# Three engines of a hybrid decoder layer put in written order while its mixers run

## The chip, the cores and the metric

One core of one Trainium2 chip runs one launch of the kernel. The metric is device time in microseconds. A profile of one execution stands beside the times.

## The reference

The layer works on 2048 tokens of width 1024 in float32. Cut to what matters:

```python
hn = rms_norm(h, pre_mix_norm)
proj = hn @ w_in                      # q, k, v, z, a, b of DeltaNet; f, i, q, g of HGRN2
q, k, v = silu(causal_conv4(qkv))     # then l2norm of q and k
o_a = gated_delta_rule(q, k, v, g_dec, beta)     # 4 heads of 128, chunks of 64
o_b = hgrn2(silu(q_hg), (1 - lb) * sigmoid(-f), i_hg, log_f)   # 4 heads, chunks of 16
mix = concat(head_norm(o_a) * silu(z), head_norm(o_b) * silu(g))
h = h + rms_norm(mix @ w_out)
h = h + rms_norm(square(relu(rms_norm(h) @ w_up)) @ w_down)
h = h + rms_norm(p @ w_ple_proj) * sigmoid(h @ w_gate)
```

## The kernel before, in words

Every float32 operand of a big matmul is split into two parts (`split`, L163: a copy on ScalarE at L165, a difference on VectorE at L166), and three products of the parts make one matmul of full precision.

The function `trunk` has four stretches. The first (L361 to L404) multiplies half of the tokens' embeddings p by w_ple (`embed_tile`, L297), stores the tiles (L304, `ed`), and makes the split operands xt of the first quarter of the tokens. The second, the mixers (L407 to L1084), is what the change touches. The third is the output projection, and the fourth the MLP and the gated embedding; in both TensorE runs one long list of matmuls (L1102 and others).

In the mixers the tokens are cut into 4 quarters q of 512. For each quarter TensorE runs 33 *works* (L1019 to L1038): `ab` (the decays and betas of all heads) and, for each of 4 heads, 8 projections of 128 columns. A work is 24 matmuls of 128x512 (L1033) on a weight tile w, and is cut into 3 *ticks* of 8 matmuls. All that the mixers do besides is written as Python generators: `gdn_mixer` (DeltaNet), `hgrn_mixer`, `conv_silu`, `finish` (head norm), `x_scale` and `load_x` (the next quarter's operands, with the split), `decays`, `down_sums` (sums of weights for the MLP). Tables of numbers (`A_STEPS`, `B_STEPS` and others, L51 to L67) say at which tick, or half tick, a generator is resumed; `tick()` (L349) and `half()` (L354) resume what the agenda holds. One head has a period of 24 ticks. What a generator issues between two yields therefore stands, in the program as written, between two groups of matmuls.

The kernel is built under a scheduler that can reorder each engine's instructions. TensorE is in written order for the whole kernel (L306, `tc.manual_schedule`), and so is SyncE, which issues the DMAs, inside the first stretch (L361) and the works' loop (L1013). Before the change ScalarE, VectorE and GpSimd are ordered by the scheduler everywhere: it may take an instruction whose operands are ready ahead of one that was written earlier.

The names that the steps below use:

- DeltaNet, one head: `e_g` (L590, VectorE) and its exponentials (L588, L592, L593, ScalarE) give the decay matrix of the *next* head, while the *previous* head's chain over 4 chunks runs: psa (L735, TensorE), r_g (L737, VectorE), psb (L740, TensorE), w_g (L742, ScalarE), psc (L745, TensorE), S_g (L747, VectorE), then psa of the next chunk.
- The *solve* (L669, L672, L674, VectorE): 32 rows of small triangular systems, two rows at a step of three instructions, each of which needs the one before; two steps are written per tick.
- Its inverse is then doubled in size: xn_g (L688, VectorE), psp_g (L693, TensorE).
- HGRN2: qk_h, att_h, gg_h (L791 to L837, VectorE), keys_h (L829, ScalarE), at_h (L824, TensorE), S_h (L851, VectorE), pss_h (L849, TensorE).
- Ahead of the works' loop stand memsets of the mixers' tiles on VectorE: bound (L419), um, part and xt_full (L424), eight states S (L428).
- `decays` (L465) makes gb from the work `ab` and, by way of gbb (L487) and ps_gb (L490), the columns that the DeltaNet heads need.
- For q = 0 each weight tile is loaded into one of two buffers `raw` (L455), split, and kept in DRAM (L181); later quarters reload it already split (L186).
- At a change of quarter, 9 ticks ahead of it, `load_x` (L944 on) scales (L954) and splits eight tiles xt; the work `ab` of the next quarter and its `decays` follow.
- After the last work (L1041 to L1043) two tiles w_pleb of w_ple and four operands pT (two tiles for each of the quarters 2 and 3, loaded through two buffers `ld` of the pool m2) are made, and 16 more embed tiles (mme, L192) fill TensorE while the last head's mixers end (L1046 to L1084).

Of the kernel before, what the change touches and what calls it, by code (L numbers as in the profile page):

```python
# [84 lines left out]
def trunk(ctx, tc, x, xT, pT, vecs, w_in, w_ab, gdn_a_log, gdn_dt_bias, w_out, w_up, w_down,  # L85
# [321 lines left out]
    with mixers as mctx:  # L407
        mp = mctx.enter_context(tc.tile_pool(name="mp", bufs=1))
        m2 = mctx.enter_context(tc.tile_pool(name="m2", bufs=2))

        def flat(t):
            return t.rearrange("p a b -> p (a b)")
# [1338 lines left out]
```

## Time and profile before

| | us |
|---|---|
| median of 3 runs | 2759.96 |
| lowest and highest run | 2754.35 and 2760.57 |
| profiled execution, its own time | 2759.13 |
| its span | 2757.3 |
| TensorE busy in the span | 2673.0 |
| VectorE busy | 2046.0 |
| ScalarE busy | 1469.8 |
| GpSimd busy | 104.2 |

The span runs from the first to the last instruction that the profiler recorded; 1.8 us of the execution's own time lie around it. A busy time is the union of an engine's recorded instructions, so overlapping ones count once. In rows of a timeline the first number is the start in us from the span's start, the second the time taken; in square brackets stand the engine's idle time ahead of that instruction and what ended it. The mixers lie between about 45 and 1100 us of the span.

### The profile page before, as it was taken

The numbers are of one execution on the slowest core, as the hardware profiler recorded it, in microseconds if no ns is written. First come the engines' busy times: TensorE is split into PE (matmuls) and PEld (weight loads), VectorE is DVE, ScalarE is ACT, GpSimd is POOL, SyncE is SP. The second block draws the span as 40 slices with busy tenths as digits, with TensorE's granted clock in tenths as the row PEclk, the third lists the DMA queues.
The fourth block names the chain that finished last, engine by engine and source line by source line (L and its number), as shares of the span: only waits on it lengthen the run. The fifth ranks groups of instructions, "written<-read, shape, count | busy, mean of one in ns | idle before, by whom it ended". The sixth has DMA issues, their size and how long they took to land.

```text
span 2757.3 us, 38414 instructions
## 1 busy us (share of the span) xinstructions
PE 2673.0 (97%) x12745; PEld 2221.0 (81%) x12745; DVE 2046.0 (74%) x4245; ACT 1469.8 (53%) x2944; POOL 104.2 (4%) x104
## 2 busy tenths in 40 slices
PE   7999999999999999999899999999999999999999
PEld 5788788888888888777788887887888888887887
DVE  6788877787778777577888867767787765567776
ACT  6665554455546445666555645555455555465421
POOL 0000000000000000000000000001000000001000
PEclk9999999999999999999999999999999999999999
DMA  7776776666766665787466547667464446577664
GB/s 263 260 245 219 233 250 221 222 219 233 239 213 217 200 213 169 260 302 238 160 226 220 187 146 253 220 196 244 148 216 139 158 167 209 192 253 244 208 210 133
DMA packets 268742, 589.24 MB, mean 214 GB/s; under 512 B 55658, under 2 KB 60232, under 8 KB 249344
## 3 DMA queue, kind: packets, MB, share of 16 engines
q1 hardware_dynamic: 268544, 586.79, 63.7%
q8 instruction: 101, 1.65, 0.3%
q14 instruction: 97, 0.79, 0.1%
HBM read 419.75 MB, written 166.92 MB: 213 GB/s over the span
## 4 chain that ended last, share of the span: by engine, by line
PE 63%; DVE 10%; DMA 8%; issue 5%; ACT 4%; SPq 1%; POOL 1%; DVEq 0%; POOLq 0%; ACTq 0%
PE u L1102 21%; PE d L1102 19%; PE mm L1033 11%; PE mmg L1102 6%; DMA ud_g<-u_g 1%; DMA sys_g<-ud_g 1%; PE mmo L1102 1%; DVE pr_g L669 1%; DVE xs_g L672 1%; DMA raw_out<-in_w_out_dram 1%; DVE xs_g L674 1%; DVE raw_xt L954 1%; DMA db<-hid 1%; DVE xt L166 1%; DMA b<-h1d 1%
## 5 line engine op out<-in xcount | busy, mean ns | idle before, releaser
L1033 PE MATMUL mm<-xt,w 128*128 128x512 f32 x3072 | 785.5, 402 | 1.3 <-ACT zt_zg L548 0.7
L1033 PEld LDWEIGHTS mm<-xt,w 128*128 128x128 f32 x3072 | 558.8, 190 | 107.0 <-ACT zt_zg L548 1.1
L1102 PE MATMUL d<-db,da 128*128 128x512 f32 x2688 | 613.5, 390 | 5.8 <-DVE db L219 3.2
L1102 PE MATMUL u<-t,wu 128*128 128x512 f32 x2604 | 593.3, 390 | 3.5 <-ACT wu L165 3.4
L1102 PEld LDWEIGHTS d<-db,da 128*128 128x128 f32 x2688 | 503.9, 188 | 114.7 <-DVE db L219 6.3
L1102 PEld LDWEIGHTS u<-t,wu 128*128 128x128 f32 x2604 | 489.6, 188 | 106.5 <-ACT wu L165 4.2
L219 DVE TENSOR_TENSOR db<-db 128x512 fp32r<-128x512 f32 x224 | 161.5, 721 | 76.7 <-ACT db L218 75.8
L1431 DVE TENSOR_TENSOR u<-u,u 128x512 f32<-128x512 f32 x224 | 150.7, 684 | 60.0 <-PE u L1102 58.1
L218 ACT ACTIVATE db<-db 128x512 fp32r<-128x512 f32 x224 | 140.8, 629 | 85.1 <-DMA db<-hid 81.8
L1102 PE MATMUL mmo<-mixT,w_out 128*128 128x512 f32 x720 | 170.5, 398 | 9.7 <-DVE w_out L166 6.2
L1102 PE MATMUL mmg<-h2T,wg 128*128 128x512 f32 (+1 forms) x792 | 174.7, 383 | 0.0
L1102 PEld LDWEIGHTS mmo<-mixT,w_out 128*128 128x128 f32 x720 | 137.8, 192 | 41.3 <-DVE w_out L166 7.9
L1102 PEld LDWEIGHTS mmg<-h2T,wg 128*128 128x128 f32 x792 | 145.5, 188 | 29.1
L1472 ACT ACTIVATE u<-u 128x512 f32<-128x512 f32 x128 | 80.9, 632 | 165.1 <-DVE u L1431 164.7
L166 DVE TENSOR_TENSOR da<-da 128x512 fp32r<-128x512 f32 x128 | 93.0, 726 | 87.2 <-ACT da L165 86.8
L165 ACT ACTIVATE da<-da 128x512 fp32r<-128x512 f32 x128 | 80.5, 629 | 135.6 <-DMA da<-sumd 109.8
L165 ACT ACTIVATE wu<-a 128x512 fp32r<-128x512 f32 x124 | 73.9, 622 | 53.0 <-DMA a<-in_w_up_dram 50.2
L669 DVE TENSOR_TENSOR pr_g<-xs_g,sys_g 128x16 f32<-128x16 f32 (+14 forms) x240 | 93.9, 391 | 5.4
L229 POOL TENSOR_TENSOR acc_y<-acc_y,sq_y 128x512 f32<-128x512 f32 x28 | 38.4, 1370 | 1381.7 <-ACT sq_y L228 1381.7
L166 DVE TENSOR_TENSOR wu<-a,wu 128x512 fp32r<-128x512 f32 x124 | 85.0, 688 | 4.3 <-ACT wu L165 4.3
L1473 ACT ACTIVATE u<-u 128x512 f32<-128x512 f32 x128 | 80.8, 631 | 3.7
L166 DVE TENSOR_TENSOR da<-dr,da 128x512 fp32r<-128x512 f32 x96 | 66.3, 690 | 17.6 <-ACT da L165 15.4
(374 smaller groups left out, 3810.9 us busy)
## 6 DMA issues: line engine op xcount, KB each, us to landing
w<-cache_in SPq DMA_DIRECT2D x96, 1024.0 KB
db<-hid SPq DMA_DIRECT2D x224, 256.0 KB
cache_in<-w SPq DMA_DIRECT2D x32, 1024.0 KB
hid<-u SPq DMA_DIRECT2D x128, 256.0 KB
da<-sumd SPq DMA_DIRECT2D x128, 256.0 KB
a<-in_w_up_dram SPq DMA_DIRECT2D x124, 256.0 KB
hid<-ht SPq DMA_DIRECT2D x96, 256.0 KB
dr<-in_w_down_dram SPq DMA_DIRECT2D x96, 256.0 KB
```

Source lines behind the costliest of these rows:

```text
L165: S.activation(t[:, 0], raw, AF.Copy)
L166: eng.tensor_tensor(t[:, 1], raw, t[:, 0], ALU.subtract)
L218: S.activation(t[:, 0], plain(t), AF.Copy)
L219: V.tensor_tensor(t[:, 1], plain(t), t[:, 0], ALU.subtract)
L229: eng.tensor_tensor(acc, acc, sq, ALU.add)
L669: V.tensor_tensor(pr[:, :, :, 0:i], xs[:, None, :, 0:i].broadcast_to([P, 2, GC, i]), sys[:, 0:i, i : i + 2].rearrange("p j two -> p two j" ...
L672: V.tensor_reduce(xs[:, :, i : i + 2].rearrange("p g two -> p two g"), pr[:, :, :, 0 : i + 1], AX.X, ALU.add)
L1033: PE.matmul(ps, *terms[i], start=i == 0, stop=i == nt - 1)
L1102: PE.matmul(ps, a, b, start=start, stop=stop)
L1431: V.tensor_tensor(c[new], c[old], ps, ALU.add)
L1472: S.activation(c[k], c[k], AF.Relu)
L1473: S.activation(c[k], c[k], AF.Square)
```

## The change

The three engines are put in written order from the opening of the mixers' pools to the end of the mixers, which is where the `with` of `mctx` closes:

```diff
     with mixers as mctx:
         mp = mctx.enter_context(tc.tile_pool(name="mp", bufs=1))
         m2 = mctx.enter_context(tc.tile_pool(name="m2", bufs=2))
+
+        mctx.enter_context(tc.manual_schedule(
+            engines={mybir.EngineType.DVE, mybir.EngineType.Activation, mybir.EngineType.Pool}))
 
         def flat(t):
             return t.rearrange("p a b -> p (a b)")
```

Line numbers of the changed kernel are larger by 3 from there on. TensorE's order of 11707 rows is the same; of VectorE's 4247 instructions 2433 stand elsewhere, by 8 places in the mean, and of ScalarE's 2854 there are 1113, by 1.4 places in the mean. Outside the mixers the three engines are still ordered by the scheduler. No instruction is added or taken away.

Three places on VectorE show what moves. The first is the opening of the mixers. Before, VectorE has the split of w_ab0 (the weights of the first work) among the operands of the embed tiles:

```order
L166 TENSOR_TENSOR w_plea1_346<-raw_plea1_253,w_plea1_346 128x512
L229 TENSOR_TENSOR acc_e1_364<-acc_e1_364,sq_e1_1_380 128x512
L166 TENSOR_TENSOR w_ab0_589<-raw_ab0_585,w_ab0_589 128x1024
L207 SCALAR_TENSOR_TENSOR xraw_255<-xraw_255,cols_92,rsb_x0_353 128x512 x3
L166 TENSOR_TENSOR xt0_0_368<-xraw_255,xt0_0_368 128x512
L166 TENSOR_TENSOR xt0_1_385<-xraw_255,xt0_1_385 128x512
```

In the changed kernel VectorE has it behind the last embed row (L229) and all of the memsets, with the splits of the second and third weight tile and of the norm's operand hl_e0 after it:

```order
L229 TENSOR_TENSOR acc_e1_364<-acc_e1_364,sq_e1_7_538 128x512
L422 MEMSET bound_557 128x36
L427 MEMSET um5_559 128x256
...
L431 MEMSET S6_0_581 128x128
L431 MEMSET S7_0_583 128x128
L166 TENSOR_TENSOR w_ab0_591<-raw_ab0_587,w_ab0_591 128x1024
L166 TENSOR_TENSOR w_4_0_0_596<-raw_4_0_0_589,w_4_0_0_596 128x1024
L166 TENSOR_TENSOR w_0_0_0_599<-raw_0_0_0_594,w_0_0_0_599 128x1024
L166 TENSOR_TENSOR hl_e0_615<-acc_e0_288,hl_e0_615 128x512
L474 MEMSET gb_0_640 36x512
```

The three weight splits moved from ahead of the memsets to behind them, and hl_e0 moved behind all three. On SyncE the loads of w_0_0_0's and w_8_0_0's raw tiles and the store of w_ab moved behind the last of the 16 stores of `ed`.

The second place is one head of the steady part, the last head of quarter 2, where VectorE's e_g2_3 belongs to the next DeltaNet head and S_h2_1 is the state of an HGRN2 head. Before, on VectorE:

```order
L669 TENSOR_TENSOR pr_g2_2_7993<-xs_g2_2_7994,sys_g2_2_7948 128x8x12
L587 TENSOR_TENSOR tail_g2_3_8049<-gf_g2_3_8001,gcol_2_6278 128x4
L590 TENSOR_TENSOR e_g2_3_8053<-gf_g2_3_8001,cst_89 128x512
L851 SCALAR_TENSOR_TENSOR S_h2_1_0_8038<-S_h1_1_3_5306,gg_h2_1_6_7940,pss_h2_1_0_8036 128x128
L672 TENSOR_REDUCE xs_g2_2_7994<-pr_g2_2_7993 128x2x4
L674 SCALAR_TENSOR_TENSOR xs_g2_2_7994<-xs_g2_2_7994,sys_g2_2_7948 128x4
```

In the changed kernel VectorE has there:

```order
L675 TENSOR_REDUCE xs_g2_2_7996<-pr_g2_2_7995 128x2x4
L677 SCALAR_TENSOR_TENSOR xs_g2_2_7996<-xs_g2_2_7996,sys_g2_2_7950 128x4
L672 TENSOR_TENSOR pr_g2_2_7995<-xs_g2_2_7996,sys_g2_2_7950 128x8x10
L675 TENSOR_REDUCE xs_g2_2_7996<-pr_g2_2_7995 128x2x4
L677 SCALAR_TENSOR_TENSOR xs_g2_2_7996<-xs_g2_2_7996,sys_g2_2_7950 128x4
L590 TENSOR_TENSOR tail_g2_3_8051<-gf_g2_3_8003,gcol_2_6280 128x4
L593 TENSOR_TENSOR e_g2_3_8055<-gf_g2_3_8003,cst_89 128x512
L750 SCALAR_TENSOR_TENSOR S_g2_1_1_8080<-S_g2_1_0_7984,cd_g2_1_6703,psc_g2_1_1_8078 128x128
L854 SCALAR_TENSOR_TENSOR S_h2_1_1_8086<-S_h2_1_0_8040,gg_h2_1_6_7942,pss_h2_1_1_8084 128x128
```

Tail and e_g moved from ahead of S_h of chunk 0 to behind it and behind the solve steps of their own tick (up to row 10 of the system); S_g and S_h of chunk 1 now stand ahead of the next solve steps.

The third place is the end of the last work. Before, VectorE has the splits of w_pleb and pT among the solve of the last head (pr_g3_3, xs_g3_3), for example:

```order
L674 SCALAR_TENSOR_TENSOR xs_g3_3_11454<-xs_g3_3_11454,sys_g3_3_11408 128x4
L166 TENSOR_TENSOR w_pleb0_11663<-raw_pleb0_11639,w_pleb0_11663 128x512
L669 TENSOR_TENSOR pr_g3_3_11453<-xs_g3_3_11454,sys_g3_3_11408 128x8x16
L166 TENSOR_TENSOR w_pleb0_11663<-raw_pleb0_11639,w_pleb0_11663 128x512
L851 SCALAR_TENSOR_TENSOR S_h3_2_0_11494<-S_h2_2_3_8811,gg_h3_2_6_11400,pss_h3_2_0_11492 128x128
```

In the changed kernel VectorE has all eight of them in one piece, behind the last r_g of head 2 and the solve's last steps:

```order
L740 SCALAR_TENSOR_TENSOR r_g3_2_3_11631<-vt_g3_2_10695,inv_g3_2_10517,psa_g3_2_3_11629 128x128
...
L677 SCALAR_TENSOR_TENSOR xs_g3_3_11456<-xs_g3_3_11456,sys_g3_3_11410 128x4
L672 TENSOR_TENSOR pr_g3_3_11455<-xs_g3_3_11456,sys_g3_3_11410 128x8x30
L675 TENSOR_REDUCE xs_g3_3_11456<-pr_g3_3_11455 128x2x4
L677 SCALAR_TENSOR_TENSOR xs_g3_3_11456<-xs_g3_3_11456,sys_g3_3_11410 128x4
L166 TENSOR_TENSOR pT2_0_11647<-raw_pT2_0_11645,pT2_0_11647 128x512
L166 TENSOR_TENSOR pT2_1_11652<-raw_pT2_1_11650,pT2_1_11652 128x512
L166 TENSOR_TENSOR pT3_0_11657<-raw_pT3_0_11655,pT3_0_11657 128x512
L166 TENSOR_TENSOR pT3_1_11662<-raw_pT3_1_11660,pT3_1_11662 128x512
L166 TENSOR_TENSOR w_pleb0_11665<-raw_pleb0_11641,w_pleb0_11665 128x512 x2
L166 TENSOR_TENSOR w_pleb1_11670<-raw_pleb1_11643,w_pleb1_11670 128x512 x2
```

The four pT splits and the four half splits of w_pleb moved behind r_g of chunk 3, whose psa TensorE issues after its last in-projection matmul, and the order among them turned: pT first, w_pleb last.

## The prediction

> **What bounds the kernel now.** The page's busy times come first, then its chain of work that ended last, then a table of the mixers by stretches, then what TensorE waited for between 64 and 1150 us.
>
> ```profile
> PE 2673.0 (97%) x12745; PEld 2221.0 (81%) x12745; DVE 2046.0 (74%) x4245; ACT 1469.8 (53%) x2944; POOL 104.2 (4%) x104
> PE 63%; DVE 10%; DMA 8%; issue 5%; ACT 4%; SPq 1%; POOL 1%; DVEq 0%; POOLq 0%; ACTq 0%
> 64.00:1087.00 1023.00, 996.75 (x5389) 846.70 (x5390) 784.44 (x2250) 550.32 (x1418) 55.66 (x64) 0.99 0.68 226
> PE psc_g L745 <- ACT w_g L742: 14.9, 13, 4.5
> PE psp_g L693 <- DVE xn_g L688: 5.0, 4, 2.1
> PE psa_g L735 <- DVE S_g L747: 3.6, 4, 1.9
> PE ps_gb L490 <- DVE gbb L487: 2.8, 1, 2.8
> PE at_h L824 <- ACT keys_h L829: 2.3, 3, 0.9
> ```
>
> TensorE is busy for 97% of the span and carries 63% of the last chain. The third line is the steady part of the mixers: of 1023 us TensorE is busy for 996.8, VectorE for 784.4, ScalarE for 550.3. So TensorE bounds, and only 26.2 us of idle time are there to be won. The waits below it say which chains come late: above all psc for ScalarE's w_g, once per DeltaNet head. TensorE's order does not change, so the new order of the others can act in one way only: it makes TensorE wait at other places, or for other lengths. VectorE has about 24% of slack in this stretch as a mean. The question is where it has none.
>
> **The start.** The timeline around the first mixer work:
>
> ```profile
> 39.45 1.21 DVE L166 TENSOR_TENSOR w<-raw,w 128x1024 fp32r<-128x1024 f32 x1
> 44.81 1.62 SPq L304 DMA_DIRECT2D ed<-e  x2
> 45.32 5.74 PE L1033 MATMUL mm_ab<-xt,w_ab 128*128 128x512 f32 x24 [0.31 <-ACT sq_e L228]
> 51.23 0.09 DVE L419 MEMSET bound<- 128x36 f32 x1 [2.06 <-DMA ed<-e]
> 52.93 1.15 DVE L428 MEMSET S<- 128x128 f32 x8
> 52.66 0.33 SPq L456 DMA_DIRECT2D raw<-in_w_in_dram  x1
> 59.75 1.04 ACT L165 ACTIVATE w<-raw 128x1024 fp32r<-128x1024 f32 x1
> ```
>
> TensorE goes from the embed tiles into mm_ab at 45.32 almost without a pause (0.31), because w_ab was split long before. The memsets begin at 51.23, since their memory is free only when the last embed store has landed, and end at 52.93 + 1.15 = 54.08, so they take 2.85. In the new order the split of w_ab stands behind them. The last two stores are issued from 44.81 to 46.43; they may land sooner than 51.2, as weight loads and a store of w_ab no longer go ahead of them. I put the first memset midway between 46.4 and 51.2, at 48.8. Then w_ab is split at 48.8 + 2.85 + 1.2 = 52.85, and mm_ab begins **7.5 us late** (5.1 to 9.9 by the two ends). Behind it on VectorE stands the split of w_0_0_0, whose load can start only when w_ab has left its buffer, at 52.85, and behind that hl_e, which TensorE wants right after mm_ab, at 52.85 + 5.74 = 58.6. From a load's issue at 52.66 to its copy at 59.75 there are 7.1 us, so a load takes between 0 and 7.1; I take 4. With 1.04 for the copy, 1.21 for the split and 0.7 for hl_e it is 59.8: 1.2 more (0 to 4.3). With the clock (below, 1.7) the start costs **+10.4**, between 5 and 16.
>
> **The clock.** A wait also costs time after it:
>
> ```profile
> 319.70 0.71 PE L693 MATMUL psp_g<-xn_g,um 128*128 128x128 f32 x4 [2.10 <-DVE xn_g L688]
> 320.00:322.00 2.00, 2.00 (x13) 0.63 1.31 51
> 322.00:324.00 2.00, 2.00 (x6) 0.52 0.37 141
> 428.02 0.80 PE L745 MATMUL psc_g<-w_g,kt_g 128*128 128x128 f32 x2 [4.55 <-ACT w_g L742]
> ```
>
> The longest wait was that of psc at 428.02, 4.55 us. But already after one of 2.10 us the granted clock was 0.63 and then 0.52 for two stretches of 2 us: 2 x 0.37 + 2 x 0.48 = 1.7 us of work lost. I charge 1.7 to a long wait, and to a part of those near 2 us. The Trainium skill, "TensorE: Matmul & The Clock Gate", section "HAM oscillation — how this bites in real kernels", puts the abstract rule at no idle gaps of TensorE over about 3.4 us. The trace differs, since here 2.10 us were enough. By that rule the six charges of 1.7 that stand on waits of 2 to 3 us below would fall away, and the sum would come out at about 2808.
>
> **The steady heads.** The last head of quarter 2 in the timeline:
>
> ```profile
> 750.24 0.31 DVE L669 TENSOR_TENSOR pr_g<-xs_g,sys_g 128x80 f32<-128x80 f32 x1
> 751.13 0.33 DVE L669 TENSOR_TENSOR pr_g<-xs_g,sys_g 128x96 f32<-128x96 f32 x1
> 751.45 0.68 DVE L590 TENSOR_TENSOR e_g<-gf_g,cst 128x512 f32<-128x512 f32 x1
> 752.06 0.34 DVE L851 SCALAR_TENSOR_TENSOR S_h<-S_h,gg_h,pss_h 128x128 f32<-128x128 f32 x1
> 752.17 1.28 ACT L592 ACTIVATE e_g<-e_g,gcol 128x128 f32<-128x128 f32 x4 [0.40 <-DVE e_g L590]
> 753.88 0.34 ACT L742 ACTIVATE w_g<-psb_g,cc_g 128x128 f32<-128x128 f32 x1
> 754.28 0.49 PE L745 MATMUL psc_g<-w_g,kt_g 128*128 128x128 f32 x2 [0.56 <-ACT w_g L742]
> ```
>
> VectorE's e_g at 751.45 releases four exponentials on ScalarE; w_g stands behind them in ScalarE's queue, and psc came 0.56 late for it. In the new order e_g stands behind S_h and two solve steps of its own tick. A step takes 751.13 - 750.24 = 0.89, so e_g can come up to 1.8 later, and psc with it; where VectorE had idled and does the steps sooner, nothing is lost. I take 1.2 for each of 12 heads (it is nearer to the full delay, as the solve is what VectorE does at that time), 14.4, and 1.7 of clock in three of them: **+19**, between 0 and 12 x (1.8 + 1.7) = 42.
>
> In return S_g and S_h of the next chunk stand ahead of solve steps. What that can bring is bounded by the waits of psa for S_g (3.6), of psp for xn (5.0) and of at_h for keys (2.3), 10.9 in all. I take half, **-6**.
>
> **The three changes of quarter.** A table by stretches of 12 us around the first full one:
>
> ```profile
> 276.00:288.00 12.00, 10.48 (x57) 8.34 (x55) 7.96 (x30) 3.65 (x8) 0.00 (x0) 1.00 0.87 283
> 288.00:300.00 12.00, 11.64 (x68) 9.56 (x67) 11.90 (x32) 6.36 (x15) 0.00 (x0) 1.00 0.70 221
> 300.00:312.00 12.00, 12.00 (x59) 9.87 (x57) 12.00 (x33) 4.83 (x11) 0.00 (x0) 1.00 0.76 239
> 312.00:324.00 12.00, 9.90 (x46) 7.91 (x46) 8.79 (x26) 8.62 (x16) 1.01 (x1) 0.86 0.65 153
> ```
>
> Here VectorE has no slack: 11.90 and 12.00 of 12 us are busy (third column of busy times), with the scale and split of eight tiles xt beside the solve. The scheduler had a choice of what to let wait; in written order an xt split, a solve step and an r_g each wait for all that was written ahead, and in 312 to 324 the decays' chain between VectorE and ScalarE (8.79 and 8.62 busy) blocks what stands behind it. In 276 to 288 VectorE idles for 4.0 us. If work that it ran ahead there returns to its place, the backlog is 4 us larger, and the idle 3.2 us of 312 to 324 lie inside chains that now can't be filled. I take 5.3 of additional wait and 1.7 of clock: 7 for each of three changes, **+21**. The ends are 0 (TensorE's tolerance of a tick or two takes it up) and 15 each (twice the 7.3 us that VectorE idles in these rows: once lost where it had run ahead, once more in the chains), 45.
>
> **The end.** The timeline at the last in-projection work:
>
> ```profile
> 1065.42 12.96 SPq L205 DMA_DIRECT2D raw_pT<-in_pT_dram  x3
> 1076.24 0.69 DVE L166 TENSOR_TENSOR pT<-raw_pT,pT 128x512 fp32r<-128x512 f32 x1
> 1080.82 1.33 ACT L165 ACTIVATE pT<-raw_pT 128x512 fp32r<-128x512 f32 x2
> 1085.54 2.07 PE L1033 MATMUL mm<-xt,w 128*128 128x512 f32 x8
> 1087.45 0.38 PE L735 MATMUL psa_g<-S_g,y_kg 128*128 128x128 f32 x2
> 1087.59 1.63 PE L192 MATMUL mme<-pT,w_pleb 128*128 128x512 f32 x6
> 1089.58 0.60 DVE L669 TENSOR_TENSOR pr_g<-xs_g,sys_g 128x240 f32<-128x240 f32 x1
> 1090.09 0.35 DVE L737 SCALAR_TENSOR_TENSOR r_g<-vt_g,inv_g,psa_g 128x128 f32<-128x128 f32 x1
> ```
>
> The first embed matmul follows at 1087.59 without a wait: pT and w_pleb had been split since 1071. In the new order they stand behind r_g, which needs psa of 1087.45. So r_g ends at 1087.45 + 0.38 + 0.35 = 1088.2. Two solve steps at full width follow: 0.89 each above at an L669 of 0.31, here 0.60, so about 1.25 each, until 1090.7. Two splits of pT2 at 0.66 end at 1092.0. Only they free the buffers for the other two loads; the last issue ended at 1065.42 + 12.96 = 1078.38 and the copies began at 1080.82, so a load takes at most 2.4. I take 2.2: 1094.2, then ScalarE's copy 0.65, the split 0.7, and two half splits of w_pleb0 at 0.7: 1097.0. That is 9.4 us after 1087.59, and 1.7 of clock: **+11**, between 7 (the loads hidden) and 14 (VectorE late by one more tick of 2.1). The 16 embed tiles behind it share two buffers and two engines with the last head's chain in written places; I put **+3** on them, from -5 to +10.
>
> **The sum.** 10.4 + 19 - 6 + 21 + 11 + 3 = 58.4. The profiled execution took 2759.1 (its span of 2757.3 and 1.8 around it), 0.8 below the median of the runs. Its time and the sum give 2817.5, rounded to **2818**. GpSimd's 104 us are on no queue that matters here, and its order moves hardly at all; I charge nothing.
>
> **Rivals.** *Only the two ends cost.* The steady part holds because TensorE asks for results a tick or two after they are written, and VectorE's mean load of 784 in 1023 leaves 24%. For it: most waits before are under 2 us. Against it: the two rows with VectorE at 11.90 and 12.00 of 12. It gives 2759 + 10.4 + 11 = **2780**.
>
> *The lag feeds on itself.* Every head's psc comes the full 1.8 late and falls to half clock, 42, and the quarter changes cost their 45. For it: psc already waits in 13 places and once for 4.5. Against it: a longer wait of TensorE also gives VectorE time to catch up. It gives 2759 + 10 + 42 + 45 + 11 + 3, **2870**.
>
> *Faster.* VectorE's own order decides: S_g and r_g ahead of the solve end the chain that TensorE waits for. Most that this can bring is the idle 26.2 us of the steady part and, by its mean granted clock of 0.99, some 10 us of half clock. It decides if the store of the last embed tile lands before 46, so that mm_ab waits little, and if VectorE is never a tick behind. With both ends charged it gives 2759 - 36 + 21 = **2744**. Against it: psc, over half of the waits listed, waits for e_g, which moved later, not earlier.
>
> **How the numbers follow.** The forecast, all stretches a little slower, has 0.55; only the ends 0.20; the self-feeding lag 0.12; faster 0.07; and 0.06 that gains and losses cancel. A difference of 0.3%, 8.3 us, is about what a measurement of this kernel can tell from none. So slower 0.87, within it 0.06, faster 0.07. The range takes the forecast's bounds and the second case in, and the third at its edge: from 2772, which leaves room below 2780 for the lower ends of start and end (5 + 7), to 2870.
>
> **What would show it.** The first matmul of mm_ab would wait 5 to 10 us for VectorE's split of w, and in VectorE's row ahead of it the memsets would stand. The first mme behind the last mm would wait for pT or w_pleb, by about 9 us. The total of psc behind w_g would go from 14.9 to about 30; TensorE would wait for r_g, xn or gbb at the three changes of quarter, where now one wait of 2.1 stands; and more stretches would show a granted clock near 0.5. If psc's total stays near 15, the steady term is wrong; if the mixers grow by less than 25 us between their first and last mm, the quarter changes are. It would all be wrong if VectorE's waits show that the scheduler's own order had been what delayed r_g and S_g.

## The result and the profile after

The changed kernel took 2921.22 us (median of 4 runs, 2917.42 to 2927.46) against 2757.87 (4 runs, 2754.35 to 2760.57): a ratio of **1.0597**, 95% interval 1.0579 to 1.0614 (the quotient of the two medians is 1.0592). The direction was forecast, the size was not: 163 us instead of 58, and outside the range.

The profiled execution has a span of 2925.2 us, 167.9 longer. Its busy times:

```profile
PE 2725.2 (93%) x12745; PEld 2253.7 (77%) x12745; DVE 2075.5 (71%) x4245; ACT 1463.7 (50%) x2944; POOL 103.7 (4%) x104
```

TensorE has the same 12745 matmuls, but is busy for 52.2 us longer (2673.0 before): the same work at a lower clock. The other 115.7 us are idle time.

As TensorE's order is the same in all kernels here, its n-th matmul can be set against the n-th of the kernel before, and the growth of the difference of their starts says in which stretch time was lost. The profiled executions give, in us lost per stretch (borders in us of before: *start* ends at 84; *quarter* is 290 to 324, 558 to 589 and 818 to 848, about the three changes of quarter; *steady* is what lies between these, up to 1088; *first mme* is the step from the psa behind the last in-projection matmul to the second embed matmul, so that a wait of either of the first two embed matmuls falls in it; *tail* are the 55 us behind that):

| | start, to 84 | steady | quarter | first mme | tail | rest, 1143 on | sum |
|---|---|---|---|---|---|---|---|
| forecast | 10.4 | 13 | 21 | 11 | 3 | 0 | 58.4 |
| the change | 10.6 | 87.5 | 36.4 | 10.3 | 24.8 | -1.3 | 168.2 |

Start and first mme came out as worked out. Nearly all of the error is the steady heads, the tail and a part of the quarter changes. What TensorE waited for, in the whole changed kernel (waits that were as long before are left out):

```profile
PE psc_g L748 <- ACT w_g L745: 49.1, 21, 6.1
PE ps_gb L493 <- DVE gbb L490: 13.2, 4, 3.6
PE at_h L827 <- ACT keys_h L832: 12.9, 9, 7.6
PE psp_g L696 <- DVE xn_g L691: 10.9, 5, 2.6
PE psb_g L743 <- DVE r_g L740: 10.5, 7, 2.6
PE mme L192 <- ACT w_pleb L165: 9.8, 1, 9.8
PE t_hkh L546 <- DVE qk_h L829: 8.0, 1, 8.0
PE mm_ab L1036 <- DVE w_ab L166: 6.4, 1, 6.4
```

Psc's wait for w_g has gone from 14.9 to 49.1 and is still the largest, but seven others together are larger (71.7), and most of these hardly existed before. The start in the timeline:

```profile
44.83 0.73 PE L1036 MATMUL mm_ab<-xt,w_ab 128*128 128x512 f32 x2 [0.35 <-ACT sq_e L228]
47.59 0.09 DVE L422 MEMSET bound<- 128x36 f32 x1 [0.73 <-DMA ed<-e]
50.75 1.16 DVE L166 TENSOR_TENSOR w_ab<-raw_ab,w_ab 128x1024 fp32r<-128x1024 f32 x1
51.97 7.80 PE L1036 MATMUL mm_ab<-xt,w_ab 128*128 128x512 f32 x22 [6.41 <-DVE w_ab L166]
```

Two matmuls of mm_ab, which need only w's first part, go through; the third waits 6.41 for VectorE's split, and the memsets stand ahead of the split, as forecast. They began at 47.59, sooner than the 48.8 that I took. The other 22 matmuls of mm_ab took 7.80, where all 24 had taken 5.74 before.

The steady head that the forecast priced, the last of quarter 2, in the timeline of the changed kernel:

```profile
849.16 0.68 DVE L593 TENSOR_TENSOR e_g<-gf_g,cst 128x512 f32<-128x512 f32 x1
849.88 1.28 ACT L595 ACTIVATE e_g<-e_g,gcol 128x128 f32<-128x128 f32 x4 [0.40 <-DVE e_g L593]
851.58 0.35 ACT L745 ACTIVATE w_g<-psb_g,cc_g 128x128 f32<-128x128 f32 x1
851.98 0.49 PE L748 MATMUL psc_g<-w_g,kt_g 128*128 128x128 f32 x2 [2.26 <-ACT w_g L745]
852.51 0.35 DVE L750 SCALAR_TENSOR_TENSOR S_g<-S_g,cd_g,psc_g 128x128 f32<-128x128 f32 x1 [2.66 <-PE psc_g L748]
```

The chain is closed: e_g late on VectorE, four exponentials and gf on ScalarE, w_g behind them, psc behind w_g, and VectorE itself idle for 2.66 with S_g, with the next solve steps ready behind it. Before, this psc had waited 0.56, so that it waits 1.70 longer. The same wait of 2.26 stands in six heads (psc at 415.23, 488.53, 714.69, 851.98, 1011.39 and 1146.00). In one of them it is a gain: the psc of 488.53 is the one that had waited 4.55 before. And it did not always cost the clock: behind four of the six the granted clock was at 0.50 within 1.5 us, as behind 415.23, while behind 488.53 and 1011.39 it stayed at 1.00 (TensorE's busy time, then the granted clock):

```profile
416.00:419.00 3.00, 3.00 (x10) 0.50 0.02 8
489.00:494.00 5.00, 5.00 (x33) 1.00 0.31 84
```

The four steady stretches as a whole, before and after:

```profile
84.00:290.00 206.00, 197.61 (x1055) 1.00 0.74 245
324.00:558.00 234.00, 226.24 (x1232) 0.99 0.70 234
589.00:818.00 229.00, 226.31 (x1250) 1.00 0.69 233
848.00:1087.00 239.00, 236.16 (x1298) 0.99 0.64 214
```

```profile
94.00:326.00 232.00, 207.86 (x1059) 0.95 0.67 219
371.00:623.00 252.00, 230.84 (x1228) 0.97 0.63 211
667.00:922.00 255.00, 237.97 (x1252) 0.96 0.61 206
965.00:1222.00 257.00, 243.96 (x1301) 0.97 0.58 189
```

The same matmuls, to within five, take 920.6 us of busy time instead of 886.3, so **34 us of the steady loss are the clock**, at a mean of 0.95 to 0.97; the idle time went from 21.7 to 75.4, which is the other 54.

A change of quarter, the first of three alike:

```profile
355.96 1.28 ACT L479 ACT_TABLE_LOAD   x1
357.92 0.68 DVE L480 SCALAR_TENSOR_TENSOR sp<-sp,se 4x512 f32<-4x512 f32 x1 [2.78 <-ACT se L479]
360.49 0.42 DVE L691 STREAM_TRANSPOSE xn_g<-xt_g 128x256 f32<-128x256 f32 x1
360.96 1.12 PE L696 MATMUL psp_g<-xn_g,um 128*128 128x128 f32 x4 [2.59 <-DVE xn_g L691]
366.77 0.28 DVE L490 COPY gbb<-gb 36x256 f32<-36x256 f32 x1
367.11 0.32 PE L493 MATMUL ps_gb<-cst,gbb 36*128 36x36 f32 x1 [3.05 <-DVE gbb L490]
```

```profile
355.00:361.00 6.00, 3.41 (x16) 1.00 0.01 2
361.00:371.00 10.00, 6.45 (x20) 0.51 0.80 236
```

VectorE stands 2.78 us with sp, for ScalarE's exponential and logarithm, and 1.28 of this is the ACT_TABLE_LOAD that ScalarE has between the two; xn, which needs neither, stands behind it, and TensorE waits 2.59 for xn, runs at half clock, and waits 3.05 for gbb, which is a short copy behind a convolution and steps of an HGRN2 head. The tail:

```profile
1232.04 2.93 PE L192 MATMUL mme<-pT,w_pleb 128*128 128x512 f32 x6 [9.75 <-ACT w_pleb L165]
1244.31 0.63 ACT L218 ACTIVATE mixT<-mixT 128x512 fp32r<-128x512 f32 x1 [5.74 <-DMA mixT<-mixd]
1250.45 0.42 ACT L832 ACTIVATE keys_h<-qk_h 128x256 f32<-128x256 f32 x1 [1.95 <-DVE qk_h L829]
1250.92 1.22 PE L827 MATMUL at_h<-qk_h,keys_h 128*128 128x128 f32 x4 [7.59 <-ACT keys_h L832]
```

The first embed matmul waits 9.75 (forecast 9.4). Then ScalarE stands 5.74 us with the copy of a mixT tile whose load was issued in the same step, and the last head's keys, in the same queue, come 7.59 late.

### The profile page after: what moved, and what is told of

Its sections match the earlier page's. It is cut to its first block, busy times and chain, and to the rows that moved or that the text cites. A ratio compares the mean times of both kernels' runs of the same rounds, so it can differ in the third digit from the quotient of the medians.

```text
span 2925.2 us, 38388 instructions
## 1 busy us (share of the span) xinstructions
PE 2725.2 (93%) x12745; PEld 2253.7 (77%) x12745; DVE 2075.5 (71%) x4245; ACT 1463.7 (50%) x2944; POOL 103.7 (4%) x104
## 4 chain that ended last, share of the span: by engine, by line
PE 50%; DVE 4%; DMA 4%; issue 3%; ACT 3%; POOL 1%; SPq 0%; POOLq 0%; DVEq 0%; ACTq 0%
PE u L1105 20%; PE d L1105 18%; PE mmg L1105 6%; PE mm L1036 3%; DMA mixT<-mixd 1%; PE mmo L1105 1%; DMA da<-sumd 0%; DMA raw_out<-in_w_out_dram 0%; POOL acc_y L229 0%; DVE t L166 0%; PE mme L192 0%; DMA xo<-in_xT_dram 0%; DVE w_out L166 0%; DMA b<-h1d 0%; DVE b L1252 0%
## 5 line engine op out<-in xcount | busy, mean ns | idle before, releaser
L1036 PE MATMUL mm<-xt,w 128*128 128x512 f32 x3072 | 806.1, 410 | 2.9 <-ACT qk_h L772 2.9
L1036 PEld LDWEIGHTS mm<-xt,w 128*128 128x128 f32 x3072 | 575.0, 195 | 113.2 <-ACT qk_h L772 3.4
L1105 PE MATMUL mmo<-mixT,w_out 128*128 128x512 f32 x720 | 169.4, 396 | 11.2 <-DVE w_out L166 6.4
L832 ACT ACTIVATE keys_h<-qk_h 128x256 f32<-128x256 f32 x80 | 33.4, 417 | 145.2 <-DVE qk_h L829 144.8
L229 POOL TENSOR_TENSOR acc_y<-acc_y,sq_y 128x512 f32<-128x512 f32 x28 | 38.9, 1389 | 1382.4 <-ACT sq_y L228 1381.6
```

The lines of the kernel that those rows point to most:

```text
L229: eng.tensor_tensor(acc, acc, sq, ALU.add)
L832: S.activation(keys.rearrange("p (n a s) -> p a n s", a=2, s=2 * s), side(k, QT, 2 * s, False), AF.Copy)
L1036: PE.matmul(ps, *terms[i], start=i == 0, stop=i == nt - 1)
L1105: PE.matmul(ps, a, b, start=start, stop=stop)
```

## The experiments

Twelve kernels were run, all beside runs of the kernel before on the same chip. TensorE's order is that of before in every one. The table has what each lost per stretch, measured as above:

| | start | steady | quarter | first mme | tail | time, us | ratio, 95% |
|---|---|---|---|---|---|---|---|
| the change | 10.6 | 87.5 | 36.4 | 10.3 | 24.8 | 2921.22 | 1.0579 to 1.0614 |
| e1 VectorE only | 11.3 | 29.2 | 45.6 | 4.3 | 27.1 | 2876.01 | 1.0404 to 1.0435 |
| e2 ScalarE only | 1.0 | 20.5 | 3.4 | 6.9 | 21.4 | 2809.5 | 1.0160 to 1.0190 |
| e3 states late | 10.9 | 91.6 | 28.8 | 8.6 | 36.6 | 2937.56 | 1.0625 to 1.0660 |
| e4 steady only | 1.1 | 86.2 | 36.4 | 0.0 | 1.4 | 2877.62 | 1.0412 to 1.0443 |
| e5 e_g behind w_g | 12.4 | 49.2 | 34.8 | 9.7 | 25.3 | 2886.35 | 1.0436 to 1.0467 |
| e6 before, e_g later | 0.5 | -4.7 | -1.4 | 0.0 | 0.5 | 2753.87 | 0.9957 to 0.9981 |
| e7 loads ahead | 12.0 | 85.0 | 36.3 | 10.3 | 15.4 | 2913.22 | 1.0536 to 1.0567 |
| e8 norm op later | 11.8 | 97.1 | 34.2 | 9.7 | 26.2 | 2938.09 | 1.0626 to 1.0662 |
| e9 five places | 2.4 | 52.7 | 25.9 | 0.0 | 19.7 | 2864.0 | 1.0343 to 1.0395 |
| e10 without GpSimd | 11.3 | 86.8 | 35.0 | 10.3 | 24.6 | 2923.35 | 1.0564 to 1.0618 |
| e11 decays later too | 2.0 | 57.1 | 15.1 | 0.0 | 20.8 | 2850.6 | 1.0312 to 1.0342 |
| e12 before, two moves | -1.1 | -3.0 | 0.6 | 0.0 | 0.5 | 2754.46 | 0.9973 to 0.9993 |

The theory formed on the two traces, V, was that VectorE in written order stands still with r_g, S_g and S_h while TensorE makes their operand. Rival S put the loss on ScalarE's order.

**e1 and e2, one engine alone.**

```diff
-            engines={mybir.EngineType.DVE, mybir.EngineType.Activation, mybir.EngineType.Pool}))
+            engines={mybir.EngineType.DVE}))
```

and for e2 `{mybir.EngineType.Activation}`.

> VectorE alone in written order, ScalarE and GpSimd left to the scheduler. Theory V (the loss is VectorE's: in written order each of its waits for TensorE holds ready solve work behind it): most of the 163 us stays, 2880 to 2930. Theory S (the loss is ScalarE's: w_g and the keys stand behind long runs of copies and exponentials): under 30 us stays, below 2790. If both orders are needed for the loss, 2800 to 2860.

> ScalarE alone in written order. Theory V: 2755 to 2790, since ScalarE's rows moved by 1.4 places in the mean. Theory S: 2850 to 2930.

Measured 2876.01 and 2809.5, so neither theory has the loss alone: VectorE's order costs about 115 us, a little under what theory V gave, ScalarE's 48. Start and quarter changes are VectorE's; with ScalarE left to the scheduler the quarter changes cost even more, 45.6 against 36.4. But the steady heads cost 29.2 and 20.5 alone, and 87.5 together: **38 us belong to the two orders together**. What TensorE waited for behind w_g, in e1 and then in e2:

```profile
PE psc_g L748 <- ACT w_g L745: 1.5, 2, 1.1
```

```profile
PE psc_g L748 <- ACT w_g L745: 26.1, 14, 5.9
```

With ScalarE left to the scheduler the wait all but vanishes (14.9 before). With VectorE left to it, it is 26.1, not 49.1. One order takes 13.4 us from it, the other adds 11.2, and both together add 34.2. So that wait needs both: e_g late on one engine, and w_g behind its exponentials on the other. In e1 the scheduler let w_g by; the head of above there:

```profile
814.66 0.37 ACT L745 ACTIVATE w_g<-psb_g,cc_g 128x128 f32<-128x128 f32 x1 [1.73 <-PE psb_g L743]
815.72 1.28 ACT L595 ACTIVATE e_g<-e_g,gcol 128x128 f32<-128x128 f32 x4 [0.40 <-DVE e_g L593]
```

The tail goes the other way: each order alone costs nearly what both cost. Over the whole kernel the two losses, 115 and 48, come to what both orders cost together beside the same runs, 160: what the steady heads lose more, the tail and the quarter changes lose less.

**e3, states written half a tick behind their matmul.**

```diff
-                V.scalar_tensor_tensor(r, vt[:, c, :], inv[:, c : c + 1], psa, ALU.mult, ALU.subtract)
+                soon(partial(V.scalar_tensor_tensor, r, vt[:, c, :], inv[:, c : c + 1], psa, ALU.mult, ALU.subtract))
...
+        def soon(fn):
+            def once():
+                fn()
+                yield
+            at(clock[0] + 0.5, once(), (0,))
```

S_g and S_h likewise.

> All three engines in written order as in the change, but r_g, S_g and S_h are written half a tick (four matmuls) behind the matmul that they read, so that a solve step or two stand ahead of them and VectorE does not stand still while TensorE makes their operand. Theory V: the steady heads win back a good part of their 88 us, time 2840 to 2890, and VectorE's waits for psc, psa and pss fall from 138 us to under 70. Theory S, and a theory that the states only come later by this: 2915 to 2960.

Measured 2937.56: slower, as expected if the states only come later by this, and theory V gets no support. VectorE's waits in the mixers fell as it said, from 138.2 to 42.1 for the three together. The row of S_g in the change, and in e3:

```profile
DVE S_g L750 <- PE psc_g L748: 67.0, 34, 3.2
```

```profile
DVE S_g L918 <- PE psc_g L748: 18.8, 20, 1.8
```

But TensorE's waits did not go, they moved:

```profile
PE psa_g L738 <- DVE S_g L918: 48.7, 23, 6.1
PE psc_g L748 <- ACT w_g L745: 11.0, 9, 2.7
```

Psa now waits 48.7 for S_g (3.6 in the change), psc 11.0. The state stands behind solve steps now, and TensorE waits for the state. As the edit does both at once, it does not show what the standing still cost by itself.

**e4, the opening and the tail left to the scheduler.**

```diff
+            steady = ExitStack()
             for j, (name, key, src, q, h, then, g, b) in enumerate(works):
+                if j == 3:
+                    steady.enter_context(tc.manual_schedule(engines={
+                        mybir.EngineType.DVE, mybir.EngineType.Activation, mybir.EngineType.Pool}))
...
+                if j == len(works) - 1:
+                    steady.close()
```

> The three engines in written order only from the fourth work's first tick to the end of the last work; the opening and the tail behind the last work are left to the scheduler. By the comparison of the two traces the start costs 10.6, the first embed matmul 10 and the tail behind it 23: without them 2875 to 2890. If the tail's loss comes from a backlog of the last head and not from the order there, 2895 to 2910.

Measured 2877.62: start, first mme and tail are gone (1.1, 0.0, 1.4), and steady heads and quarter changes stand as in the change (86.2, 36.4). The opening does not hand its loss on to the steady heads, nor these theirs to the tail, so these can be studied apart, and the tail's loss is made in the tail.

**e5 and e6, e_g half a tick later,** in the change and in the kernel before:

```diff
-A_AHEAD = (-8, -6)
+A_AHEAD = (-8, -5.5)
```

> The change, with the next head's e_g step (VectorE's tail and e_g, ScalarE's four exponentials) written half a tick later, so that ScalarE has w_g of chunk 1 ahead of the exponentials. Theory Q (the steady heads' loss is this queue: e_g late on VectorE, and w_g behind its exponentials on ScalarE): psc's waits for w_g fall from 49 to under 15, and with the clock 40 us come back, 2870 to 2890. Theory L (VectorE is behind in general, and another wait takes the place): psc's waits fall, but the time stays over 2905.

> The kernel before (all three engines left to the scheduler), with e_g written half a tick later in the same way. ScalarE's queue then has one of the four exponentials ahead of w_g instead of four and gf. Theory Q: psc's waits of 14.9 fall to under 6 and the long one's half clock goes, 2740 to 2752. Theory L: 2755 to 2765.

In e5 ScalarE has w_g of chunk 1 ahead of the exponentials. Measured 2886.35, in the range of theory Q: the steady loss fell from 87.5 to 49.2, by 38.3. That is as much as the two orders had cost together and not alone, but these need not be the same microseconds: psc's waits for w_g fell by 32.8, while those for r_g grew from 10.5 to 14.8 and those of nrm for hl_g from 3.6 to 10.6. The rows of e5, then of e6:

```profile
PE psc_g L748 <- ACT w_g L745: 16.3, 11, 4.3
PE psb_g L743 <- DVE r_g L740: 14.8, 10, 4.3
PE nrm_g L265 <- ACT hl_g L165: 10.6, 10, 3.2
```

```profile
PE psc_g L745 <- ACT w_g L742: 8.9, 12, 1.6
```

In the kernel before the same line is a small gain: **2753.87 against 2761.84**, ratio 0.9969 (0.9957 to 0.9981), above the 2740 to 2752 of theory Q. Psc's waits fell to 8.9, not under 6, and the longest from 4.5 to 1.6, so that the half clock behind it went too.

**e7, loads ahead of their splits in the tail.**

```diff
-        for k in range(KD):
+        def load(k):
             t = next_pool().tile([P, 2, QT], F32R, tag="ring", name=f"mixT{q}_{k}")
             nc.sync.dma_start(plain(t), mixd[q][k])
-            split_in_place(t)
             xin[q].append(t)
+        ahead = 3 if q == 0 else 1
+        for k in range(ahead):
+            load(k)
+        if ahead > 1:
+            yield
+        for k in range(KD):
+            split_in_place(xin[q][k])
+            if k + ahead < KD:
+                load(k + ahead)
...
-            at(clock[0], mix_operands(0), (1, 2, 3, 4, 6, 7, 9, 11))
+            at(clock[0], mix_operands(0), (1, 4, 5, 6, 7, 8, 9, 10, 12))
```

> The change, with the loads of mixT behind the last work issued three tiles ahead of their splits and the first split three ticks later. Theory D (in the tail ScalarE and VectorE stand still for a load that is written right ahead of its split, and the last head's keys stand behind it): the tail behind the first mme loses 5 to 12 us instead of 25, 2900 to 2912. If the tail's loss is the half clock and the last head's own chain: 2915 to 2925.

Measured 2913.22. The tail's loss fell by 9.4, to 15.4; time and tail are a little above what theory D gave. The wait for the keys in that place and the longest one of the tail, that of t_hkh for qk_h, are now:

```profile
1245.74 1.22 PE L837 MATMUL at_h<-qk_h,keys_h 128*128 128x128 f32 x4 [3.46 <-ACT keys_h L842]
PE t_hkh L556 <- DVE qk_h L839: 3.3, 1, 3.3
```

They were 7.59 and 8.0. The held load is shown; it is a part of the tail, not all of it.

**e8, VectorE's operation of the head norm one tick later,** as VectorE stood still for its load in the change:

```profile
DVE m_g L275 <- DMA m_g<-sd_g: 27.1, 13, 4.3
```

```diff
-           + (50, 52, 54, 56, 57, 58, 60, 61))
+           + (50, 52, 54, 57, 58, 59, 61, 62))
```

> The change, with VectorE's operation on m_g in the DeltaNet head norm (and what follows it) written one tick later, so that VectorE does not stand still for the load of m_g, 27 us in 13 places. If standing still there delays what TensorE waits for, 10 to 25 us come back, 2895 to 2912. If the slack around takes it up, 2915 to 2925.

Measured 2938.09, slower than the change by 17, or by 13 when each is set against its own runs of before; neither side expected it. VectorE no longer waits for m_g, but for the loads of the next step (7.2 and 2.2 us in the change):

```profile
DVE og_h L567 <- DMA rsb_h<-rd_h: 31.3, 13, 5.0
DVE og_g L567 <- DMA rsb_g<-rd_g: 20.2, 9, 3.6
```

The larger one belongs to the HGRN2 head, whose steps were not moved: the DeltaNet norm's chain of loads and stores now stands ahead of its load in SyncE's queue. That reading is from the rows; it was not tried apart.

**e9, five places written differently,** all three engines in written order: e5 and e7; the memsets of the mixers' tiles gathered in a function clear() behind the first two weight splits; the second half of the decays 1.5 ticks later, with gbb's copy right behind its scans and ahead of a convolution; and pT and w_pleb as below:

```diff
-        V.memset(bound, 0.0)
...
             split_work(0)
+            split_work(1)
+            clear()
             stage_work(2)
-            split_work(1)
...
             S.activation(se, se, AF.Ln, bias=1.0)
+            yield
             V.scalar_tensor_tensor(sp, sp, 0.0, se, ALU.max, ALU.add)
...
-            yield
-            nc.sync.dma_start(gd, gb[0:4, :])
-            yield
             back = mt(f"gbb_{q}", "gbb", 1, (36, QT // 2))
             V.tensor_copy(back.rearrange("p (n b i) -> p n b i", b=NB, i=SB), odd_back(gb))
+            yield
+            nc.sync.dma_start(gd, gb[0:4, :])
+            yield
...
+                if j == len(works) - 1:
+                    ple = [stage_ple(i, f"pleb{i}") for i in range(2)]
+                    pts = {2: [operand(ra, pT[blk(k), tok(2)], f"pT2_{k}", stage=m2) for k in range(2)]}
+                    ple[0] = ple[0](V)
...
-                        at(clock[0], decays(ps, q), (0, 2, 4, 5))
+                        at(clock[0], decays(ps, q), (0, 1.5, 2, 4, 5))
```

> All three engines in written order, with five places written differently: e_g half a tick later and the mixT loads ahead, as in two runs before; the memsets behind the first two weight splits; VectorE's second half of the decays 1.5 ticks behind its first half, and gbb right behind the scans instead of behind a convolution; the first w_pleb and the pT of quarter 2 made ahead of the last work. Theory H (in each place one written instruction stands still for ScalarE, a load or memory and holds ready work behind it): start 11 falls to 0 to 4, the three quarter changes 36 to under 18, the first mme 10 to under 2, the tail 25 to about 15, the steady heads 88 to about 49 as before: 2825 to 2850. Theory B (at the quarter changes VectorE simply has too much to do): those stay at 30 or more and the total is 2850 to 2870.

Measured 2864.0, above the 2825 to 2850 of theory H and within the 2850 to 2870 of theory B, though not with the 30 or more at the quarter changes that B gave. Start (2.4) and first mme (0.0) are as it said. The quarter changes fell only from 36.4 to 25.9 and the tail to 19.7. The waits for gbb are gone there; the one for xn is not:

```profile
PE psp_g L707 <- DVE xn_g L702: 10.5, 4, 2.9
```

The reason was the edit: at 1.5 ticks sp still stands ahead of xn in VectorE's order.

**e10, GpSimd left to the scheduler.**

```diff
+            engines={mybir.EngineType.DVE, mybir.EngineType.Activation}))
```

> VectorE and ScalarE in written order, GpSimd left to the scheduler. If GpSimd's order has no share, the time is that of the change, 2915 to 2928; if its 30 moved rows cost something (the square roots stand behind memsets that wait for a buffer), it is lower by that.

Measured 2923.35 (2922.16 to 2927.5), the time of the change and its table row: GpSimd's order has no share that shows.

**e11, sp behind xn,** as e9, and

```diff
-                        at(clock[0], decays(ps, q), (0, 1.5, 2, 4, 5))
+                        at(clock[0], decays(ps, q), (0, 3, 3.5, 4, 5))
```

> As the run with five places mended, but VectorE's second half of the decays (sp, the scans, gbb) is written three ticks behind its first half, so that it stands behind xn. Theory H (xn stands still behind sp, which waits 2.8 for ScalarE's exponential and logarithm): TensorE's wait of 2.9 for xn at each of the three quarter changes falls under 0.7 and they cost 13 to 18 instead of 26, 2845 to 2858. Theory B (VectorE has too much to do there, whatever its order): another wait takes its place, 2858 to 2868.

Measured 2850.6, with the quarter changes at 15.1, both in the range of theory H. The two waits:

```profile
PE ps_gb L504 <- DVE gbb L498: 3.9, 4, 1.0
PE psp_g L707 <- DVE xn_g L702: 0.3, 1, 0.3
```

So some 20 of the 36 us at the quarter changes were two short instructions held by the order: xn behind sp, which waited for ScalarE (10.8, from e9 to here), and gbb behind a convolution (about 9, from e5 to e9, which changed other places too). What is left is about 5 at each change, with waits for r_g and S_g of about 1 us each; whether that is VectorE's backlog was not tried.

**e12, the kernel before with e_g later and gbb behind the scans** (the two edits above):

> The kernel before, with e_g half a tick later (as in an earlier run) and gbb written right behind the scans. The scheduler then has gbb ahead of one convolution step instead of behind it. If the first changes of the decays are on the path, 2 to 4 us under the run with e_g alone: 2749 to 2752. If not, 2752 to 2756; both are under the kernel before.

Measured 2754.46 (ratio 0.9983, 0.9973 to 0.9993): still below the kernel before, and no better than e6. The second move brings nothing that shows.

## Why the prediction was wrong

**The start (+10.4; measured 10.6)** held in its mechanism; that the size came out so closely is in part luck. The wait was 6.41 instead of 7.5 and that of 1.2 for hl_e right behind mm_ab did not come, while the half clock cost more than 1.7 (22 matmuls in 7.80), and a later wait of 2.4 for hl_e was not foreseen.

**The end (+11; measured 10.3)** held: the wait of 9.75 against 9.4. The chain ran as told as far as the load; its last link was not VectorE's half splits but ScalarE's copies of the second pT and of w_pleb, of about the same length. The half clock behind the wait falls in the tail.

**The steady heads (+19 and -6; measured 87.5)** are the step that failed: its one cost was mis-sized, and other costs of the two orders had no term. "I take 1.2 for each of 12 heads" priced one wait by the delay of one instruction on VectorE, 1.8 at most. The wait it named did grow, by 34.2 instead of 14.4: to 49.1, where about 30 was to show it. In the head that it looked at the growth was 1.70, inside the 1.8; but elsewhere psc waited up to 6.1, so that 1.8 was no upper end, since w_g also stands behind the exponentials on ScalarE in written order, where the scheduler let it by in e1 (1.5 us of such waits). e5 gave back 38 us by moving this step alone: 38 in 12 heads is 3.2 a head, with its half clock. The other 49 us had no term. In e5 they are 29 us of idle time, in many waits of 0.5 to 4 us, for r_g, hl, gg and cc above all, and 20 us of busy time by the clock. VectorE's and ScalarE's orders cost 29 and 20 each for itself, which is as much, but that it is the same loss is not shown: ScalarE's alone has 26.1 us of psc's waits for w_g in it. The -6 for S_g ahead of the solve was not to be seen: psa's waits for S_g are 3.6 in both kernels, and those for xn and keys grew. And the clock was charged three times 1.7 where it made 34 us.

**The quarter changes (+21; measured 36.4)** were mis-sized, and their reason was half right. The prediction named backlog and the decays' chain together. e11 shows the order of two short instructions, xn behind the chain and gbb behind a convolution, as some 20 of the 36; at most the other 15 are left for backlog, and no run shows that they are it.

**The tail (+3; measured 24.8)** failed in its mechanism: it was looked at as two buffers shared by written places. What it missed is that each split of mixT is written in the step that issues its load, so that two engines stand still for a DMA with the last head's chain behind them. e7 shows some 9 us of it.

**The clock.** Here the trace bears on the rule of the Trainium skill that the prediction weighed ("TensorE: Matmul & The Clock Gate", "HAM oscillation — how this bites in real kernels", no idle gaps over about 3.4 us): the granted clock was 1.00 up to the end of the wait of 2.59 at 360.96 and 0.51 in the 10 us behind it, so a shorter gap than that was enough, and the charge stood on the right side. A gap of 2.26 was enough in four of six places. The charge should have been larger: eight times 1.7, 13.6 us, against 52.2 of the 167.9.

**Of the rivals,** "the lag feeds on itself" (2870) came nearest and was given 0.12. Its number is nearer by its larger prices; that a lag fed on itself is not shown. e4 shows that the opening handed nothing on to the steady heads, nor these to the tail; from head to head it was not tried. "Faster" fell with the direction. "Only the two ends cost" is refuted by e4 from the other side: with both ends taken away, 117 us stay.

**What stays open.** The 49 us of the steady heads that e5 leaves, the 15 of the quarter changes and the rest of the tail are known by the waits in the trace, not by an edit that takes each away. e8 was one try at it, and moved the wait elsewhere.

## What to carry to other kernels

Written order on an engine that has a quarter of slack is not free: what counts is not how busy an engine is, but what stands behind each of its instructions that waits, for another engine, a load, or memory. Price a pair of orders together, since a result that is late on one engine and held in the queue of the next costs more than the two apart (87.5 against 49.7 in the steady heads), though elsewhere two waits may hide one another, as in the tail here. And look for the useful half of such a change: the one move that the written order showed, e_g behind w_g, made the kernel before faster by 0.2 to 0.4%.

## What the runs showed of the hardware

A wait of 2.59 us on TensorE was followed by a granted clock of 0.51 for 10 us, in which a second wait of 3.05 lies; of six waits of 2.26 us four were followed by 0.50 and two by 1.00. The whole change cost 52.2 us of busy time in the same 12745 matmuls, nearly a third of the loss: here short waits on TensorE cost more than their length, though not each of them.
